# A two-layer encoder trunk: the loads of x wait for the first weights, idle products stand around the last column sums, and the last factor is broadcast into two banks

## The chip, the core and the metric

The kernel runs on one core of one Trainium2 chip. The metric is the device time of one execution in microseconds (us). A core has a matrix engine (TensorE, "PE" in the profile, its weight loads "PEld"), a vector engine (VectorE, "DVE"), a scalar engine (ScalarE, "ACT"), a general engine (GpSimd, "POOL"), and an engine that only issues transfers (SyncE, "SP"). ACT and POOL issue transfers too, from the same instruction stream in which their other work stands; a "q" behind an engine's name (SPq, ACTq, PEq) means this stream. All transfers of the core run on the same 16 DMA engines, in queues: q1 holds what SP issues, q10 what ACT issues.

## The reference

The model width is D = 2048, the sequence S = 256, and there are two layers. Cut to what matters here:

```python
h = x
for i in range(2):
    u = rmsnorm(h, norm_g[i]) @ w_in[i]               # conv group, attention group, gates
    ya, yb = conv_group(u), window_attention(u)       # each times its own gate
    h = h + concat([ya, yb]) @ w_out[i]
    e = rmsnorm(p[i] @ w_pe[i], pe_g[i])              # per-layer embedding, p[i] is (256, 256)
    h = h + e * sigmoid(h @ w_pg[i])
return rmsnorm(h, final_g)

def rmsnorm(x, g):
    return x * rsqrt(mean(x * x, axis=-1) + 1e-6) * g
```

## The kernel before

Activations lie transposed in memory: 128 channels on the partitions, then 16 channel tiles, then the 256 sequence positions. Weights come from memory in half chunks of 512 KB (128 partitions x 1024 floats) in the order in which they are used; two halves make one buffer `raw`, and there are three such buffers. The large products split each weight into a rounded part and a remainder (L163 on ACT, L166 on DVE) and use three passes (L394, L395, L396). The program order on TensorE, VectorE and ScalarE is the order of the code ("manual" order). The order on SP, on POOL and between the transfer queues is set by a planner, which also gives every transfer a semaphore that its landing raises.

The start, which the change touches. VectorE clears a tile `zeros`, and TensorE runs four products on it (`warm`, L256, two instructions each). SP issues `p` (256 KB, L260), then the first weights in seven pieces (L269): the first half in two pieces of 256 KB (`load_half(0, 0, 2)`), the second, third and fourth half in one each; then `gains`, the fifth and sixth half, and small tables. ScalarE runs a small activation `first` (L279) ahead of which its function table is loaded, and issues the four loads of x (512 KB each, L272, queue q10).

TensorE then computes `e = p[0] @ w_pe[0]` straight from the raw weights (L490): eight banks of eight instructions each. The first two banks need the first half (one 256 KB piece each), the next two the second half, and so on. Between the banks ScalarE squares x two tiles at a time (L377, L380, L498), VectorE adds the squares into `hacc` (L381) and folds them at the end (L368), and ScalarE copies each bank of e out (L514). After the fifth bank, `rstd_col` (L343) sums the squares over the channels: products with x's squares as the weights and a column of ones, which give one number per position. DVE scales it (L346), POOL raises it to the power -1/2 (L348), DVE puts it on a diagonal (L353), and `rstd_row` (L359) multiplies a matrix of ones with that diagonal, which broadcasts the factor to all partitions (`rh0b`). The sixth bank of e lies between the two on TensorE. VectorE multiplies x by its gain and this factor (L463, `hn`), ScalarE and VectorE split that into `hg` (L466, L467), and the first large product `ag` begins.

The end, which the change touches too. The last gate product `g` ends; ScalarE and VectorE form the last tile of h and its square (`sq`, L807); `rstd_col` sums over `hparts`, two parts: the folded squares of the tiles before, and this last square. Three products on constants (`warm2`, L845) stand between `rstd_col` and `rstd_row`. The factor `rb` stays in the PSUM bank: VectorE multiplies six of the eight pairs of output tiles by it straight from the bank (L853), ScalarE copies it to `rbs` for POOL (L855), which can't read PSUM and does the other two pairs. Each finished piece is sent out by SP or ScalarE (L856).

Of the kernel before, what the change touches and what calls it, by code (L numbers as in the profile page):

```python
# [12 lines left out]
AF = mybir.ActivationFunctionType  # L13
# [4 lines left out]
P = 128  # L18
D = 2048
# [106 lines left out]
def trunk_kernel(ctx: ExitStack, tc: tile.TileContext, xT, pT, wst, par, gain, relb, sinkp, onehot, out):  # L126
    nc = tc.nc
# [18 lines left out]
    def bank(name):  # L146
        return ps.tile([P, 2, S], F32, tag="ps", name=name)
# [3 lines left out]
    raws, spl = {}, {}  # L151
# [100 lines left out]
    zeros = wk.tile([P, S], F32, name="zeros", tag="sq", bufs=3)  # L252
    nc.vector.memset(zeros, 0.0)
    wb = bank("warm")
# [21 lines left out]
    load_half(0, 0, 2)  # L276

    first = wk.tile([P, 2], F32, name="first", tag="rv")
    nc.scalar.activation(first, zeros[:, 0:2], AF.Square)  # L279
    for k in range(0, KT, 4):  # L280
        load_x(k)
    load_half(0, 1)
# [16 lines left out]
    ident = cst.tile([P, P], F32, name="ident")  # L299
    make_identity(nc, ident)  # L300
    ones = cst.tile([P, P], F32, name="ones")
# [33 lines left out]
        return t  # L335


    def rstd_col(parts, dim, name, between=None):

        c = bank(name + "c")  # L340
        for x, a in enumerate(parts):
            for b in range(2):
                nc.tensor.matmul(c[:, 0, b:b + 1], a[:, b * P:(b + 1) * P], ones[:, 0:1],  # L343
                                 start=(x == 0 and b == 0), stop=(x == len(parts) - 1), skip_group_check=True)
        v = wk.tile([P, 2], F32, name=name + "v", tag="rv")
        nc.vector.tensor_scalar(v, c[:, 0, 0:2], 1.0 / dim, EPS, ALU.mult, ALU.add)  # L346
        col = wk.tile([P, 2], F32, name=name + "col", tag="rcol")
        nc.gpsimd.tensor_tensor(col, v, mhalf, ALU.pow)  # L348
        if between:
            between()  # L350
        dg = wk.tile([P, 2, P], F32, name=name + "dg", tag="rdg", bufs=1)
        for b in range(2):
            nc.vector.tensor_scalar(dg[:, b, :], ident, col[:, b:b + 1], None, ALU.mult)  # L353
        return dg

    def rstd_row(dg, name, tag="rb", copy=True):

        bb = bank(name + "b")
        nc.tensor.matmul(bb[:, 0, :], ones, dg.rearrange("p a b -> p (a b)"), start=True, stop=True)  # L359
        if not copy:  # L360
            return bb[:, 0, :]
        rb = wk.tile([P, S], F32, name=name + "rb", tag=tag, bufs=1)
        nc.scalar.copy(rb, bb[:, 0, :])
        return rb

    def fold(a):
        t = wk.tile([P, S], F32, name="fold", tag="sg")
        nc.vector.tensor_add(t, a[:, 0, :], a[:, 1, :])  # L368
        return t

    def halves_of(a):
        return [a[:, 0, :], a[:, 1, :]]
# [74 lines left out]
    for l in range(DEPTH):  # L447
# [5 lines left out]
        rbs, subs = [], []  # L453
# [21 lines left out]
        for q in range(4):  # L475
            n = Cursor.h
# [5 lines left out]
            for jj in range(0, 4, 2):  # L482
                j = 4 * q + jj
                b = bank("e")
                for x in range(2):
                    for k in range(2):
                        if l:
                            mm3(b[:, x, :], w[:, :, jj + x, k, :], pp[:, :, k, :], x == 0 and k == 0, k == 1)
                        else:
                            nc.tensor.matmul(b[:, x, :], raw[:, jj + x, k, :], pf[:, k, :], start=x == 0 and k == 0,  # L490
                                             stop=k == 1, skip_group_check=True)
                if l == 0 and j // 2 < 4:
# [3 lines left out]
                    if j // 2 == 3:  # L496
                        sq = wk.tile([P, 2, S], F32, name="sq", tag="sq", bufs=3)
                        nc.scalar.activation(sq, h[1][:, 6:8, :], AF.Square)  # L498
                        hparts = [fold(hacc)] + halves_of(sq)
                if j // 2 == QQ[l][0]:  # L500
                    dg = rstd_col(hparts, D, f"rh{l}")
                    ahead(4 if l == 0 else Cursor.h - 1 - q + 5)
# [17 lines left out]
        def embed(l=l, eacc=eacc, e=e):  # L520

            if l == 0:
                yield from wait(8)
                bias_prep()
            for j in range(0, KT, 2):
                yield from wait(2)
                square_acc(eacc, e[j // 8][:, j % 8:j % 8 + 2, :], j == 0)
            yield from wait(6)
            es = fold(eacc)
            yield from wait(3)  # L530
            dg = rstd_col([es], D, f"re{l}")
            yield from wait(2)
            eb = rstd_row(dg, f"re{l}", "reb")
            yield from wait(50)
            while not state["enorm"]:
                yield
            for j in range(KT):
                d = e[j // 8][:, j % 8, :]
                nc.vector.scalar_tensor_tensor(d, d, pcol(l, PO_PE + j), eb, ALU.mult, ALU.mult)
                yield  # L540
# [58 lines left out]
        for q in range(4):  # L599
            n = Cursor.h  # L600
# [96 lines left out]
        def lnorm(l=l, acc=acc, za=za, ya=ya, ysum=ysum, done=done):  # L697
# [10 lines left out]
            for t in range(4):  # L708
                nc.vector.tensor_sub(q[t], q[t], bcast2(mu))
                square_acc(vacc, q[t], t == 0, nc.vector)  # L710
                if t % 2:
                    yield
            yield from wait(LY[0])
            dg = rstd_col(halves_of(vacc), W_CONV, f"rv{l}")
            yield from wait(LY[1])
            rb = rstd_row(dg, f"rv{l}")
# [106 lines left out]
        hparts = []  # L823
# [14 lines left out]
        h = e  # L838


    dg = rstd_col(hparts, D, "rf")

    wb = bank("warm2")
    for _ in range(3):
        nc.tensor.matmul(wb[:, 0, 0:P], ones, ident, start=True, stop=True)  # L845
    rb = rstd_row(dg, "rf", copy=False)
    rbs = wk.tile([P, S], F32, name="rfrb", tag="rb", bufs=1)

    for j in (0, 2, 12, 4, 6, 14, 8, 10):
        for x in [slice(0, 1), slice(1, 2)] if j == 0 else [slice(0, 2)]:  # L850
            d = og[j // 8][:, j % 8:j % 8 + 2, :][:, x, :]
            eng, r = (nc.gpsimd, rbs) if j >= 12 else (nc.vector, rb)
            eng.tensor_mul(d, d, r.unsqueeze(1).broadcast_to(d.shape))  # L853
            if j == 0 and x.start == 0:
                nc.scalar.copy(rbs, rb)  # L855
            (nc.scalar if j >= 12 or j % 4 == 0 and x.start == 0 else nc.sync).dma_start(out[:, j:j + 2, :][:, x, :], d)  # L856


# [75 lines left out]
```

## Time and profile before

| | us |
|---|---|
| median of three runs | 983.94 (983.38 to 984.1) |
| the profiled execution | 983.99 |
| its span, from the first to the last instruction | 982.2 |
| around the span | 1.8 |
| TensorE busy | 965.8 |
| VectorE busy | 774.6 |
| ScalarE busy | 560.0 |
| GpSimd busy | 86.6 |

The mean granted clock of TensorE is 0.992 of full speed. A row of the timeline has the start in us, the length in us, the engine, the line, the operation, what is written and read, and a count where several instructions stand merged in one row; brackets at its end hold the idle time before it and what ended it. A row of a stretch has its length, the busy time of each engine with the number of its instructions, the granted clock ("PEclk"), the mean busy share of the DMA engines and GB/s.

### The profile page before, as it was taken

To read this page: it belongs to the slowest core of one execution; us is meant where nothing else is said; L and a number is where in the kernel's file an instruction comes from. 1 tells how busy PE (TensorE), PEld (TensorE's weight loads), DVE (VectorE), ACT (ScalarE), POOL (GpSimd) and SP (SyncE) were. 2 spreads that over 40 slices of the span, in tenths; PEclk is the share of its full clock that TensorE was granted. 3 is DMA by queue.
4 is the path that set the end of the run, shared out by engine and by line. 5 is a ranking of instruction groups with operands and counts; after the bars stand their busy time and mean duration, and the time that the engine had idled before them with its cause. 6 is when DMAs were issued, how large, how long until landed. Compare 5 with 4: busy or idle time off the path is not lost.

```text
span 982.2 us, 18152 instructions
## 1 busy us (share of the span) xinstructions
PE 965.8 (98%) x7438; PEld 925.5 (94%) x7438; DVE 774.6 (79%) x1319; ACT 560.0 (57%) x862; POOL 86.6 (9%) x87
## 2 busy tenths in 40 slices
PE   8999999999999999999999999999999999999994
PEld 7999999999999999988899999999999999998884
DVE  4899989987787576687789998988887867667763
ACT  4655454777875554455566444568778545446551
POOL 0022001010000000011103200000100000100111
PEclk9999999999999999999999999999999999999997
DMA  7764636555544466446556555456454445654522
GB/s 287 254 238 171 213 131 215 189 178 181 166 153 177 149 238 225 172 172 230 198 184 237 175 203 181 172 188 204 146 168 165 172 143 200 217 191 162 197 104 86
DMA packets 29135, 182.49 MB, mean 186 GB/s; under 512 B 3723, under 2 KB 4284, under 8 KB 9212
## 3 DMA queue, kind: packets, MB, share of 16 engines
q1 hardware_dynamic: 24284, 165.17, 47.2%
q0 software_dynamic: 3472, 12.88, 4.4%
q10 hardware_dynamic: 1296, 3.28, 0.9%
q8 instruction: 58, 0.95, 0.4%
q14 instruction: 25, 0.20, 0.1%
HBM read 177.09 MB, written 4.23 MB: 185 GB/s over the span
## 4 chain that ended last, share of the span: by engine, by line
PE 97%; DVE 1%; DMA 1%; ACT 0%; POOL 0%; issue 0%; DVEq 0%; SPq 0%; ACTq 0%
PE g L391 12%; PE o L394 6%; PE o L395 6%; PE o L396 6%; PE ag L396 6%; PE ag L394 6%; PE ag L395 6%; PE g L392 6%; PE za L394 3%; PE zb L394 3%; PE q L394 3%; PE q L395 3%; PE zb L395 3%; PE za L395 3%; PE zb L396 3%; PE q L396 3%
## 5 line engine op out<-in xcount | busy, mean ns | idle before, releaser
L166 DVE TENSOR_TENSOR w<-raw,w 128x1024 fp32r<-128x1024 f32 x306 | 372.3, 1227 | 119.1 <-ACT w L163 116.1
L163 ACT CAST w<-raw 128x1024 fp32r<-128x1024 f32 x308 | 316.2, 1047 | 180.2 <-PE ag L396 45.1
L560 DVE SCALAR_TENSOR_TENSOR ac<-ac,pars 128x241 f32<-128x241 f32 (+11 forms) x480 | 217.9, 503 | 1.0
L391 PE MATMUL g<-h,w 128*128 128x512 f32 x496 | 175.3, 399 | 0.0
L396 PE MATMUL ag<-hg,w 128*128 128x256 f32 x512 | 145.2, 284 | 0.5 <-DVE w L166 0.5
L394 PE MATMUL ag<-hg,w 128*128 128x256 f32 x512 | 145.5, 284 | 0.0
L395 PE MATMUL ag<-hg,w 128*128 128x256 f32 x512 | 145.1, 283 | 0.1
L392 PE MATMUL g<-h,w 128*128 128x256 f32 x496 | 139.3, 281 | 0.0
L391 PEld LDWEIGHTS g<-h,w 128*128 128x128 f32 x496 | 93.2, 188 | 23.1
L394 PEld LDWEIGHTS ag<-hg,w 128*128 128x128 f32 x512 | 98.3, 192 | 0.9 <-ACT ac L553 0.9
L396 PEld LDWEIGHTS ag<-hg,w 128*128 128x128 f32 x512 | 98.3, 192 | 0.8 <-DVE w L166 0.7
L395 PEld LDWEIGHTS ag<-hg,w 128*128 128x128 f32 x512 | 98.3, 192 | 0.3 <-DVE hg L467 0.3
L392 PEld LDWEIGHTS g<-h,w 128*128 128x128 f32 x496 | 93.8, 189 | 0.0
L394 PE MATMUL za<-hg,w 128*128 128x256 f32 x256 | 73.7, 288 | 0.0
L394 PE MATMUL o<-yb,w 128*128 128x256 f32 x256 | 73.4, 287 | 0.0
L394 PE MATMUL q<-hg,w 128*128 128x256 f32 x256 | 73.3, 286 | 0.0
L394 PE MATMUL zb<-hg,w 128*128 128x256 f32 x256 | 73.2, 286 | 0.0
L395 PE MATMUL o<-yb,w 128*128 128x256 f32 x256 | 72.6, 284 | 0.0
L396 PE MATMUL o<-ya,w 128*128 128x256 f32 x256 | 72.5, 283 | 0.0
L394 PE MATMUL o<-ya,w 128*128 128x256 f32 x256 | 72.5, 283 | 0.0
L395 PE MATMUL o<-ya,w 128*128 128x256 f32 x256 | 72.5, 283 | 0.0
L396 PE MATMUL o<-yb,w 128*128 128x256 f32 x256 | 72.5, 283 | 0.0
(229 smaller groups left out, 2192.9 us busy)
## 6 DMA issues: line engine op xcount, KB each, us to landing
raw<-in_wst SPq DMA_DIRECT2D x153, 1024.0 KB, 4.9
bias<-fscr POOLq DMA_DIRECT2D x16, 384.0 KB, 3.8
raw<-in_wst SPq DMA_DIRECT2D x5, 512.0 KB, 9.8
x<-in_xT ACTq DMA_DIRECT2D x4, 512.0 KB, 7.1
hx<-in_xT POOLq DMA_DIRECT2D x8, 256.0 KB, 3.6
hscr<-e POOLq DMA_DIRECT2D x2, 1024.0 KB, 4.9
hx<-hscr POOLq DMA_DIRECT2D x8, 256.0 KB, 3.4
out_t<-og ACTq DMA_DIRECT2D x4, 256.0 KB, 3.0
```

What stands on the lines that cost most here:

```text
L163: nc.scalar.copy(hi, raw)
L166: nc.vector.tensor_sub(lo, raw, hi.bitcast(F32))
L391: nc.tensor.matmul(o, w[:, 0], x, start=start, stop=False, skip_group_check=True)
L392: nc.tensor.matmul(o[:, 1], w[:, 1], x[:, 0], start=False, stop=stop, skip_group_check=True)
L394: nc.tensor.matmul(o, w[:, 0], x[:, 0], start=start, stop=False, skip_group_check=True)
L395: nc.tensor.matmul(o, w[:, 0], x[:, 1], start=False, stop=False, skip_group_check=True)
L396: nc.tensor.matmul(o, w[:, 1], x[:, 0], start=False, stop=stop, skip_group_check=True)
L560: nc.vector.scalar_tensor_tensor(acc[:, t, lo_:hi_], a[:, t, lo_ + s:hi_ + s], w(k), acc[:, t, lo_:hi_], ALU.mult, ALU.add)
```

## The change

Three edits. The small activation `first` reads two elements of the first weights instead of `zeros`, so that it and all that stands behind it in ScalarE's stream wait until that piece of 256 KB has landed; the four loads of x stand right behind it. In the last norm, `rstd_col` runs five products on constants between its two parts, and four stand behind it where three stood. The factor's broadcast is made twice, into two PSUM banks: VectorE reads the one, ScalarE copies the other for GpSimd.

```diff
     first = wk.tile([P, 2], F32, name="first", tag="rv")
-    nc.scalar.activation(first, zeros[:, 0:2], AF.Square)
+    nc.scalar.activation(first, raws[0][:, 0, 0:2], AF.Square)
     for k in range(0, KT, 4):
         load_x(k)

+    def idle(n):
+        wb = bank("idle")
+        for _ in range(n):
+            nc.tensor.matmul(wb[:, 0, 0:P], ones, ident, start=True, stop=True)
+
-    def rstd_col(parts, dim, name, between=None):
+    def rstd_col(parts, dim, name, between=None, idles=0):
         c = bank(name + "c")
         for x, a in enumerate(parts):
             for b in range(2):
                 nc.tensor.matmul(c[:, 0, b:b + 1], a[:, b * P:(b + 1) * P], ones[:, 0:1],
                                  start=(x == 0 and b == 0), stop=(x == len(parts) - 1), skip_group_check=True)
+            if x == 0 and idles:
+                idle(idles)

-    dg = rstd_col(hparts, D, "rf")
-
-    wb = bank("warm2")
-    for _ in range(3):
-        nc.tensor.matmul(wb[:, 0, 0:P], ones, ident, start=True, stop=True)
+    dg = rstd_col(hparts, D, "rf", idles=5)
+    idle(4)
     rb = rstd_row(dg, "rf", copy=False)
+    rb2 = rstd_row(dg, "rf2", copy=False)
     rbs = wk.tile([P, S], F32, name="rfrb", tag="rb", bufs=1)

             if j == 0 and x.start == 0:
-                nc.scalar.copy(rbs, rb)
+                nc.scalar.copy(rbs, rb2)
```

## Prediction

> **What bounds the kernel now.** I read the page's busy times and its chain first, then the chain and the timeline of the first 25 us and of the last 20, then the transfers and the clock there.
>
> ```profile
> PE 965.8 (98%) x7438; PEld 925.5 (94%) x7438; DVE 774.6 (79%) x1319; ACT 560.0 (57%) x862; POOL 86.6 (9%) x87
> PE 97%; DVE 1%; DMA 1%; ACT 0%; POOL 0%; issue 0%; DVEq 0%; SPq 0%; ACTq 0%
> PE ag L396 <- DVE w L166: 0.5, 1, 0.5
> ```
>
> TensorE is busy 98% of the span and is 97% of the chain. The third row is from the waits of TensorE: between the start of `ag` and the last norm it lists this one and no longer one. So a delay at the start goes to the end undiminished, and the change can only move the first 25 us and the last 16.
>
> The start, from the timeline:
>
> ```profile
> 0.74 0.39 SPq L260 DMA_DIRECT2D p<-in_pT  x1
> 1.19 3.62 PE L256 MATMUL warm<-zeros 128*128 128x256 f32 x8 [1.19 <-DVE zeros L253]
> 7.07 10.56 PE L490 MATMUL e<-p,raw 128*128 128x256 f32 x40 [2.25 <-DMA raw<-in_wst]
> 14.69 0.63 ACT L380 ACTIVATE sq<-x 128x512 f32<-128x512 f32 x1
> 16.08 0.42 DVE L368 TENSOR_TENSOR fold<-hacc 128x256 f32<-128x256 f32 x1
> 17.46 0.50 PE L343 MATMUL rh0c<-ones,fold 128*128 128x1 f32 x4
> 17.82 1.03 PE L343 MATMUL rh0c<-ones,sq 128*128 128x1 f32 x8
> 18.89 0.16 DVE L346 TENSOR_SCALAR rh0v<-rh0c 128x2 f32<-128x2 f32 x1 [2.39 <-PE rh0c L343]
> 20.52 0.65 PE L359 MATMUL rh0b<-rh0dg,ones 128*128 128x256 f32 x2
> 21.01 3.62 PE L490 MATMUL e<-p,raw 128*128 128x256 f32 x16
> 24.27 0.47 PE L394 MATMUL ag<-hg,w 128*128 128x256 f32 x1
> ```
>
> The warm products end at 4.81, and TensorE waits 2.25 us for the first weights. The five banks of e take it to 17.6. The sum of squares (fold) is ready at 16.50, so here TensorE is late by about 1 us and the statistics of x are not. Behind it `rh0c`, the power, `rh0b` and `ag` follow.
>
> The transfers and the clock. The first row is the line that issues x, with the times of its first and last issue; then the queues from 1.7 to 3, from 2.7 to 13.6, from 7 to 13 (two rows) and from 13 to 15 (packets, MB, share); then from issue to landing; then stretches:
>
> ```profile
> L272 ACTq DMA_DIRECT2D x<-in_xT x4: 334/416/453, 1.2 to 7.0; - x4
> q10 hardware_dynamic: 10, 0.04, 11.1%
> q10 hardware_dynamic: 576, 2.10, 51.8%
> q10 hardware_dynamic: 344, 1.25, 52.2%
> q1 hardware_dynamic: 382, 1.21, 50.3%
> q1 hardware_dynamic: 354, 0.79, 102.9%
> x<-in_xT ACTq DMA_DIRECT2D x4, 512.0 KB, 7.1
> p<-in_pT SPq DMA_DIRECT2D x1, 256.0 KB, 2.8
> 4.53:7.94 3.41, 1.16 (x6) 0.83 (x5) 0.00 (x0) 0.61 (x2) 0.00 (x0) 1.00 0.85 269
> 7.95:11.35 3.40, 3.40 (x9) 2.65 (x9) 0.89 (x2) 1.88 (x5) 0.00 (x0) 0.50 1.03 421
> 11.35:17.60 6.25, 6.25 (x31) 5.49 (x31) 3.68 (x6) 4.85 (x9) 0.00 (x0) 1.00 1.03 405
> ```
>
> All of x (2.10 MB) moves in the 10.9 us from 2.7 to 13.6. Between 7 and 13 both queues have work and halve the bandwidth: 1.25 and 1.21 MB in 6 us, 0.21 MB per us each; q1 nearly alone, from 13 to 15, has 0.39. A stretch of 3.41 us in which TensorE was busy only 1.16 is followed by 3.4 us at clock 0.50.
>
> The end, from the timeline and two stretches:
>
> ```profile
> 966.80 0.50 PE L343 MATMUL rfc<-ones,fold 128*128 128x1 f32 x4
> 968.92 0.61 PE L343 MATMUL rfc<-ones,sq 128*128 128x1 f32 x4 [1.62 <-ACT sq L807]
> 969.39 0.92 PE L845 MATMUL warm<-ident,ones 128*128 128x128 f32 x6
> 970.55 0.48 DVE L353 TENSOR_SCALAR rfdg<-ident,rfcol 128x128 f32<-128x128 f32 x2 [0.82 <-POOL rfcol L348]
> 971.18 1.19 PE L359 MATMUL rfb<-rfdg,ones 128*128 128x256 f32 x2 [0.88 <-DVE rfdg L353]
> 972.40 0.42 DVE L853 TENSOR_TENSOR og<-og,rfb 128x256 f32<-128x256 f32 x1 [1.38 <-PE rfb L359]
> 972.86 0.37 ACT L855 COPY rfrb<-rfb 128x256 f32<-128x256 f32 x1 [3.60 <-DVE og L853]
> 973.26 3.41 DVE L853 TENSOR_TENSOR og<-og,rfb 128x256 f32<-128x256 f32 x6 [0.44 <-ACT rfrb L855]
> 973.31 2.49 POOL L853 TENSOR_TENSOR og<-og,rfrb 128x512 f32<-128x512 f32 x2 [2.80 <-ACT rfrb L855]
> 967.33:970.74 3.41, 1.38 (x10) 1.19 (x10) 1.20 (x4) 0.93 (x3) 0.71 (x1) 0.97 0.00 0
> 970.74:973.00 2.26, 1.19 (x2) 0.50 (x2) 0.71 (x3) 0.14 (x1) 0.00 (x0) 0.50 0.00 0
> 976.00:980.00 4.00, 0.00 (x0) 0.00 (x0) 0.67 (x2) 0.00 (x0) 0.00 (x0) 0.50 1.02 378
> ```
>
> TensorE is busy 1.38 of 3.41 us, and then the clock is 0.50: the broadcast takes 1.19 us where the same one at the start, at full clock, took 0.65. VectorE, ScalarE and VectorE then read one bank in turn. From 976 on the output transfers fill the DMA engines (1.02).
>
> **Part one, the loads of x.** Nothing is removed; four issues of 512 KB and all of ScalarE's stream behind `first` wait for the first 256 KB of weights. The function table is loaded ahead of `first` and stays. POOL and SP don't stand behind the wait.
>
> When do these weights land? `p`, equally large and ahead on the same queue, was issued at 0.74 and landed 2.8 later, at 3.5. Without x, q1 has the engines to itself; 256 KB more at 0.39 MB per us are 0.7 us: 4.2, and I take 4.4. Then `e` starts at the end of the warm products, 4.8 instead of 7.07, and has no gap ahead of it, so the half clock of 7.95 to 11.35 goes too. 40 instructions at 3.62/16 = 0.226 us are 9.0: the fifth bank ends at 13.9 instead of 17.6. Its later weights come in time: landed at 3.5, `p` (0.26 MB) had moved by about 3.0, so by 5.4, when x starts, q1 has moved 0.26 + 2.4 x 0.39 = 1.2 MB; it needs 1.3 MB for the third bank (at 8.4) and 1.8 MB for the fifth (at 12.0), and at 0.21 MB per us these are there at 5.9 and 8.3, half a microsecond more for the landing.
>
> What is late next is x. Issued at 4.4, its first bytes move about 1 us later, at 5.4 (an estimate: issued at 1.2, x had moved 0.04 MB by 3.0, which bounds it at 1.7). SP still has some 2.3 MB of weights queued (six halves of 0.52 MB and `p` make 3.4), so the two queues halve the bandwidth until x is through: 2.10/0.21 = 10.0 us, 15.4. In the run above the last load of x, issued at 7.0, landed 7.1 later, at about 14.05, 0.5 behind its last bytes at 13.6, so now 15.9, 1.9 later. From the second to last square (14.69) to the end of the fold (16.50) pass 1.81: the sums can begin at 15.9 + 0.1 + 1.8 = 17.8 instead of 17.46. That is +0.35, and TensorE, done at 13.9, waits 3.9 us for it.
>
> That wait has a price. As at 4.53 to 7.94, a stretch of 3.41 us with little work gives 3.4 us at half clock, and now the twelve sums (1.39 us at full clock), the sixth bank (1.8) and the broadcast lie in it. Upper bound: half clock all the way, the twelve cost 1.3 more, and the sixth bank outlasts the power chain (18.89 to 20.47) by 1 us: +2.3. Lower bound: the edge of the stretch falls such that the clock is back when the sums start: 0. I take 1.3, since only part of the 3.4 us meets work. Part one is +1.65; its ends are -1.4 (x lands when it did, the clock stays; the sums then start at 16.0) and +4 (below).
>
> The Trainium skill, "TensorE: Matmul & The Clock Gate", Part 1, has the clock halved after one idle window of about 3.4 us, and advises no idle gap over some 3 us. By the letter of that the last 1.6 us gap before 970.74 should have cost nothing; the trace shows 0.50, so the share of busy time decides here, and the measurement goes. With the letter, a wait of 3.9 us costs the same 1.3, but one of under 3 us nothing, and the sum would be 983.4.
>
> The same skill's "DMA: Bandwidth & Descriptors", Queues, rings and completion order, says that each DMA engine goes round between queues packet by packet; the 1.25 against 1.21 MB agree, and it speaks against the gain that holding x back is to bring: SP's later weights, not needed for 10 us, take half of what x then gets.
>
> **Part two, the idle products.** Five products, ten instructions at 0.92/6 = 0.15 us, are 1.5 us: from 967.3 to 968.8, inside the wait that ends at 968.92. If they ran long, each 0.1 us would be on the path. Four behind are eight instructions, 1.2 us from 969.4: 970.6, covered by the power and the diagonal up to 971.03. TensorE is then busy some 2.9 of 3.4 us, the clock stays, and the broadcast takes 0.65 instead of 1.19: -0.54. Bound from below 0, if the edge falls otherwise.
>
> **Part three, the second bank.** Two more instructions behind the first broadcast, 0.45 us, before ScalarE's copy: POOL starts at about 972.7 instead of 973.31. VectorE no longer waits for that copy (0.44) nor for turns at the bank: its second piece goes at 972.25 instead of 973.26. All but the first output are about 1.0 earlier by parts two and three together, the first 0.54. Since the transfers are the limit from 976 on, the end moves by between 0.54 and 1.0; I take 0.9.
>
> Sum against the profiled execution's own 983.99 (0.05 above the median): 983.99 + 0.35 + 1.3 - 0.9 = 984.7.
>
> **The rivals.**
>
> *Slower: x is planned behind all of SP's loads.* A transfer's issue can wait for an older landing:
>
> ```profile
> SPq L286 <- DMA raw<-in_wst: 5.4, 1, 5.4
> SPq L269 <- DMA p<-in_pT: 0.5, 1, 0.5
> ```
>
> With `p` and these `raw` pieces and x, about eight transfers were out when issues began to wait; the fourth x, too, was issued only at 7.0, when the first weights had landed. If the planner now counts SP's thirteen before x, the first x waits for the fourth `raw` half (2.4 MB, landed at about 9) and the last for the sixth, near 12.8; ScalarE's squares stand behind that. x then lands at 18 to 19.5, the sums start at 20 to 21.4: +2.5 to +4 and the clock's 1.3, less 0.9: 987.5. It decides from a first issue of x after about 6 us on. For it: the waits above. Against it: before, x was issued among SP's loads, from 1.2 on, and not behind them.
>
> *Neutral: the clock stays and x gets more than half.* Before, x moved ahead of the small-packet weights early on. If x lands near 15, the sums start at 17.0: 983.99 - 0.5 - 0.9 + some clock = 983.0.
>
> *Faster.* x lands at 14.1 and the clock stays: 983.99 - 1.4 - 0.9 = 981.7. Against it: x starts to move 2.7 us later and would need 2.10 MB in 8.2 us, 0.26 MB per us, where it had 0.21.
>
> *The idle products change nothing*, because the edge of the 3.4 us falls elsewhere: 0.5 of the gain goes, 985.2. The skill's clock page has this window run free of the kernel.
>
> **How the numbers follow.** Forecast 0.45, neutral 0.18, slower rival 0.20, idle products without effect 0.07, faster 0.10. What this measurement can tell from no change is about 0.2%, 2.0 us: faster is below 982.0, the last case and a little of neutral, 0.12; slower is above 985.9, the rival and the forecast's upper tail (half clock throughout, 985.7, and x later), 0.26; the rest, 0.62, is the same. The forecast's own range is 983.5 to 986.2. The range for 8 in 10 leaves out most of the faster case and the worst of the rival: 982.2 to 987.6.
>
> **What would show it.** In the trace after: ScalarE's issues of x at 4.2 to 4.6; `e` at about 4.8 and its first forty instructions done near 13.9; then a wait of TensorE for ScalarE or VectorE before `rh0c`, which starts between 17.3 and 18.5, at clock 0.50 for part of what follows; `ag` 1 to 2.5 us after 24.27. At the end clock 1.00 to the broadcast, `rfb` in some 0.65, VectorE's products without the gap before the second. I am wrong if `rh0c` starts before 16.8 or after 19.5, or if `rfb` still takes 1.19.

## The result, and the profile after

The changed kernel takes 990.74 us (990.55 to 991.15, five runs) against 983.94 before: 1.007 times as long, with a 95% interval of 1.0056 to 1.0084. The forecast was 984.7 with a range of 982.2 to 987.6, and no measurable difference as the likeliest outcome. The profiled execution takes 990.70, its span 988.9.

The timeline of TensorE after the change, from the start to the first large product:

```profile
1.19 3.50 PE L256 MATMUL warm<-zeros 128*128 128x256 f32 x8 [1.19 <-DVE zeros L253]
5.33 3.69 PE L498 MATMUL e<-p,raw 128*128 128x256 f32 x16 [0.65 <-DMA raw<-in_wst]
9.37 5.45 PE L498 MATMUL e<-p,raw 128*128 128x256 f32 x24 [0.35 <-DMA raw<-in_wst]
22.69 1.02 PE L349 MATMUL rh0c<-ones,fold 128*128 128x1 f32 x4 [7.87 <-DVE fold L376]
23.57 1.84 PE L349 MATMUL rh0c<-ones,sq 128*128 128x1 f32 x8
25.27 3.39 PE L498 MATMUL e<-p,raw 128*128 128x256 f32 x8
28.50 0.59 PE L367 MATMUL rh0b<-rh0dg,ones 128*128 128x256 f32 x2
...
32.20 0.47 PE L402 MATMUL ag<-hg,w 128*128 128x256 f32 x1
```

`e` starts 1.74 earlier than before (5.33 for 7.07) and its five banks end at 14.8 instead of 17.6. All of that is lost in one wait: TensorE stands 7.87 us until the fold of x's squares is there. `rh0c` starts at 22.69 instead of 17.46, 5.23 later. From `rh0c` to `ag` pass 9.51 instead of 6.81, so `ag` is 7.93 later.

ScalarE's timeline says what the fold waited for:

```profile
5.22 0.20 ACT L279 ACTIVATE first<-raw 128x2 f32<-128x2 f32 x1 [3.20 <-DMA raw<-in_wst]
5.22 6.26 ACTq L272 DMA_DIRECT2D x<-in_xT  x4
13.68 0.63 ACT L385 ACTIVATE hacc<-x 128x512 f32<-128x512 f32 x1 [8.26 <-DMA x<-in_xT]
...
20.82 0.63 ACT L388 ACTIVATE sq<-x 128x512 f32<-128x512 f32 x1 [1.05 <-DMA x<-in_xT]
```

x is issued from 5.22 on. The first load lands 8.4 us later, at 13.66, and the last at 20.74; the last squares begin at 20.82.

The queues (packets, MB, share of the DMA engines) in the stretches 5 to 8.8, 8.8 to 9 (the row of q10), 9 to 13 (two rows) and 13 to 17 (two), and the row from issue to landing:

```profile
q1 hardware_dynamic: 363, 1.23, 96.2%
...
q10 hardware_dynamic: 3, 0.01, 14.9%
...
q10 hardware_dynamic: 212, 0.82, 58.7%
q1 hardware_dynamic: 286, 0.62, 43.1%
...
q10 hardware_dynamic: 245, 0.87, 55.5%
q1 hardware_dynamic: 225, 0.75, 46.4%
...
x<-in_xT ACTq DMA_DIRECT2D x4, 512.0 KB, 9.6
```

From 5 to 8.8 there is no row of q10 at all, although x has been issued since 5.22: SP's queue has the engines alone. The first packets of x move at 8.87, 3.65 after the issue. From then to 17 the queues share as before: (0.82 + 0.87) MB in 8 us are 0.21 MB per us for x. From 17 to 20.2, to its last bytes, x has 0.40 MB, 0.13 per us, beside 0.75 MB of weights.

The clock, in the stretches 15 to 17.9, 17.9 to 22.69 and 22.69 to 28.1:

```profile
15.00:17.90 2.90, 0.00 (x0) 0.00 (x0) 1.94 (x3) 1.93 (x4) 0.00 (x0) 1.00 1.03 420
17.90:22.69 4.79, 0.00 (x0) 0.00 (x1) 2.50 (x4) 3.49 (x7) 0.00 (x0) 0.50 0.89 307
22.69:28.10 5.41, 5.41 (x19) 4.87 (x20) 1.77 (x4) 2.13 (x3) 0.70 (x1) 0.50 0.04 17
```

It is granted at 0.50 for 10 us, 5.4 of them with TensorE busy without a gap. The end, from the timeline:

```profile
974.51 0.50 PE L349 MATMUL rfc<-ones,fold 128*128 128x1 f32 x4
...
974.88 1.36 PE L342 MATMUL idle<-ident,ones 128*128 128x128 f32 x10
...
976.64 0.60 PE L349 MATMUL rfc<-ones,sq 128*128 128x1 f32 x4 [0.41 <-ACT sq L815]
...
977.11 1.14 PE L342 MATMUL idle<-ident,ones 128*128 128x128 f32 x8
...
978.90 0.67 PE L367 MATMUL rfb<-rfdg,ones 128*128 128x256 f32 x2 [0.65 <-DVE rfdg L361]
...
979.40 0.59 PE L367 MATMUL rf2b<-rfdg,ones 128*128 128x256 f32 x2
979.60 3.74 DVE L859 TENSOR_TENSOR og<-og,rfb 128x256 f32<-128x256 f32 x7 [0.85 <-PE rfb L367]
980.03 0.37 ACT L861 COPY rfrb<-rf2b 128x256 f32<-128x256 f32 x1 [3.05 <-PE rf2b L367]
...
980.48 2.49 POOL L859 TENSOR_TENSOR og<-og,rfrb 128x512 f32<-128x512 f32 x2 [2.25 <-ACT rfrb L861]
```

The broadcast takes 0.67 instead of 1.19, and VectorE's seven products go without the gap. From the first `rfc` to the end of the span pass 14.4 us (988.9 less 974.51) instead of 15.4.

So +7.7 up to the first `rfc` (974.51 for 966.80) and -1.0 behind it make the +6.7 of the two profiled executions.

One of the eleven executions of `end_only`, told below, took 2414.79 us; its ratio is worked out without it.

### The profile page after: what moved, and what is told of

Read it like the earlier page. It is cut to its first block, busy times and chain, and to the rows that moved or that the text cites. A ratio compares the mean times of both kernels' runs of the same rounds, so it can differ in the third digit from the quotient of the medians.

```text
span 988.9 us, 18181 instructions
## 1 busy us (share of the span) xinstructions
PE 968.4 (98%) x7452; PEld 928.0 (94%) x7452; DVE 774.5 (78%) x1319; ACT 559.8 (57%) x862; POOL 86.6 (9%) x87
## 4 chain that ended last, share of the span: by engine, by line
PE 95%; DMA 2%; DVE 1%; ACT 0%; SPq 0%; issue 0%; POOL 0%; DVEq 0%; ACTq 0%
PE g L399 12%; PE o L402 6%; PE o L403 6%; PE o L404 6%; PE ag L404 6%; PE ag L402 6%; PE ag L403 6%; PE g L400 6%; PE za L402 3%; PE zb L402 3%; PE q L402 3%; PE zb L403 3%; PE q L403 3%; PE za L403 3%; PE q L404 3%; PE zb L404 3%
```

## The experiments

Each is told with the median of its runs and the ratio to runs of the kernel before on the same chip, with the 95% interval; those runs had medians of 983.9 to 984.05.

### Which part loses the time

**The loads alone** (`gate_only`), the kernel before with one line changed:

```diff
-    nc.scalar.activation(first, zeros[:, 0:2], AF.Square)
+    nc.scalar.activation(first, raws[0][:, 0, 0:2], AF.Square)
```

> Part one alone: ScalarE's first activation reads the first weights, the end is that of the kernel before. Theory (the whole loss is at the start and the end gains about 1.05 us): rfc starts 7.7 us later than before, the time is 983.9 + 7.7 = 991.6. Rival (the end's edits have a part in the loss): 990.7 or less, and rfc starts less than 7 us later.

992.12 us (four runs), 1.0076 (1.006 to 1.0091). `rh0c` starts at 22.66, behind a wait of 7.64 for the fold, and the first `rfc` at 975.28, 8.5 later than before. One line is the whole loss. It is 0.8 more than in the changed kernel (7.7), since the half clock lasts until 30.53 here instead of 28.16: from `rh0c` to `ag` pass 10.70 us instead of 9.51.

**The end alone** (`end_only`): the changed kernel with `zeros` back in that line.

> Parts two and three alone; ScalarE's first activation reads zeros as before. Theory: from the first rfc to the end of the span 14.4 us instead of 15.4, the time 982.9. Rival (the gain belongs to the other phase of the clock and not to the edits): 983.9, 15.4 us.

983.02 us, 0.9992 (0.9983 to 1.0001). From the first `rfc`, at 966.80, to the end pass 14.5 us, so the end's gain is there without part one. TensorE's timeline at the start shows besides what bounds `e`:

```profile
6.97 1.97 PE L498 MATMUL e<-p,raw 128*128 128x256 f32 x8 [2.00 <-DMA raw<-in_wst]
9.67 1.99 PE L498 MATMUL e<-p,raw 128*128 128x256 f32 x8 [0.73 <-DMA raw<-in_wst]
12.19 5.45 PE L498 MATMUL e<-p,raw 128*128 128x256 f32 x24 [0.53 <-DMA raw<-in_wst]
```

Here the products run at full pace and wait for the second piece of weights and for the second half instead. They end where they ended before (17.6), where some had run at half clock: the half clock at the start of the kernel before mostly covered these landings.

**The idle products alone** (`idle_only`) **and the second bank alone** (`bank_only`), each the kernel before with part two or part three of the diff.

> Part two alone: x as before, the idle products at the end, one bank for the factor. Theory (the gain of 0.9 us in the span of the two end parts is half the clock's): clock 1.00 at rfb, rfb 0.65 instead of 1.19, VectorE's second product still waits for ScalarE's copy (0.44); from the first rfc to the end of the span 14.9 instead of 15.4, the time 983.4. Rival (all of it is the clock): 14.4, 982.9.

> Part three alone: x as before, three idle products behind the sums as before, the factor broadcast into two banks. Theory: rfb at clock 0.50 takes 1.19 as before where the clock's edge falls as before, VectorE's second product follows the first without a gap, ScalarE's copy waits for the second broadcast, some 1.2 us at half clock; from the first rfc to the end 14.9 to 15.2, the time 983.5. Rival (POOL's later start at half clock eats it): 15.4, 983.9.

`idle_only`: 983.42 us, 0.9992 (0.9984 to 1.0001); from the first `rfc` (967.94) to the end of the span (982.8) 14.9 us. VectorE's timeline, with the gap behind the first product that the shared bank makes:

```profile
973.03 0.42 DVE L858 TENSOR_TENSOR og<-og,rfb 128x256 f32<-128x256 f32 x1 [0.85 <-PE rfb L367]
973.89 3.41 DVE L858 TENSOR_TENSOR og<-og,rfb 128x256 f32<-128x256 f32 x6 [0.44 <-ACT rfrb L860]
```

`bank_only`: 983.87 us, 0.9998 (0.9989 to 1.0007); from the first `rfc` (967.04) to the end (982.4) 15.4 us, as before. Its timelines of TensorE, VectorE and GpSimd:

```profile
971.42 1.19 PE L359 MATMUL rfb<-rfdg,ones 128*128 128x256 f32 x2 [0.87 <-DVE rfdg L353]
972.40 1.06 PE L359 MATMUL rf2b<-rfdg,ones 128*128 128x256 f32 x2
...
972.64 3.74 DVE L854 TENSOR_TENSOR og<-og,rfb 128x256 f32<-128x256 f32 x7 [1.38 <-PE rfb L359]
...
973.95 2.49 POOL L854 TENSOR_TENSOR og<-og,rfrb 128x512 f32<-128x512 f32 x2 [3.19 <-ACT rfrb L856]
```

At half clock the second broadcast takes 1.06. VectorE's gap is gone, but GpSimd starts 6.9 us behind the first `rfc` instead of 6.5 before. So of the end's 0.9 to 1.0 the idle products alone bring 0.5, the second bank alone nothing that shows, and the rest comes only where the second broadcast is made at full clock. These are lengths in one profiled execution each; the intervals of the three ratios all reach 1.

### Why x came so late

**The weights held back** (`x_ahead`): the changed kernel, with the second and third pair of halves (the third to sixth half) issued only after ScalarE's four loads of x; the first, 1.31 MB with `p`, as before. SP's order is that of the code here, not the planner's.

```diff
     for k in range(0, KT, 4):
         load_x(k)
+    for c in (1, 2):
+        raws[c] = wraw.tile([P, 2, HALF], F32, tag="raw", name=f"raw{c}")
+        for x in range(2):
+            nc.scalar.activation(raws[c][:, x, 0:2], zeros[:, 0:2], AF.Square)
     load_half(0, 1)
```

> The changed kernel, but the third to sixth half of the weights are issued only once ScalarE has issued all four loads of x (small activations behind those issues write into their buffers first; SP keeps the order of the code). x is still issued at about 5.2. Theory (x stood behind the weights that SP had issued before it): x moves its first bytes within 1.7 us of its issue, x lands by 13 to 16, rh0c starts at 16 to 17.5, the time is 983.0 to 985.5. Rival (a late first issue of its queue costs 3.7 us by itself, or the halved bandwidth is all there is): first bytes at 8.9 again, rh0c not before 19, the time 987 or more.

984.72 us, 1.0006 (0.9996 to 1.0017). x is issued at 5.55 and its first bytes move at 6.58, 1.0 later: this is the delay that the prediction had taken. Its loads land from 9.97 to 16.84. The queues from 6.5 to 8 (two rows) and from 8 to 12 (two), and two rows of TensorE:

```profile
q10 hardware_dynamic: 81, 0.33, 76.4%
q1 hardware_dynamic: 23, 0.06, 10.2%
...
q10 hardware_dynamic: 351, 1.27, 98.2%
q1 hardware_dynamic: 2, 0.01, 1.8%
...
16.59 1.97 PE L502 MATMUL e<-p,raw 128*128 128x256 f32 x8 [1.51 <-DMA raw<-in_wst]
18.80 0.61 PE L353 MATMUL rh0c<-ones,fold 128*128 128x1 f32 x4 [0.24 <-DVE fold L380]
```

It is the mirror image. The weights issued from 7.97 on, behind x, move their first bytes at 11.63, land at 16.46, and now the fifth bank of `e` waits for them and ends at 18.56. `rh0c` starts at 18.80, later than I had expected (16 to 17.5): it waits for the fold, 0.24 us behind that bank, since from 12 on the weights take turns with x, whose last load lands at 16.85. So the weights' delay, with which I hadn't reckoned, doesn't set this start alone: x, too, took 10.3 us from its first bytes to its last landing.

**Another kind of queue** (`gate_pool`): x issued by GpSimd, on its software queue q0, each load behind a small copy that reads the first weights.

```diff
-        nc.scalar.dma_start(h[k // 8][:, k % 8:k % 8 + 4, :], xT[:, k:k + 4, :])
+        nc.gpsimd.tensor_copy(h[k // 8][:, k % 8, 0:2], raws[0][:, 0, 0:2])
+        nc.gpsimd.dma_start(h[k // 8][:, k % 8:k % 8 + 4, :], xT[:, k:k + 4, :])
```

> The kernel with both end parts; x is issued by GpSimd on its own queue, behind small GpSimd copies that read the first weights (so at about 5.5), and ScalarE's first activation reads zeros. SP has its weights queued as in the changed kernel. Theory (what SP has issued holds back what ScalarE issues after it; GpSimd's queue is fed another way): x moves its first bytes within 2.5 us of its issue, by 8.0, while SP's queue still moves weights, and the two then share as the prediction had it: x landed at 16.5 to 18.5, rh0c at 18.4 to 20.4, the time 985 to 988. Rival (x gets nothing until the weights issued before it are through, on whatever queue): first bytes at 8.9 or later, rh0c at 22 or more, the time 988.5 or more.

991.96 us, 1.0076 (1.0062 to 1.009), `rh0c` at 23.61: the theory that only SP's and ScalarE's queues hold each other back has fallen, and the rival's numbers came. The queues from 6 to 10, and from 10 to 11 (two rows):

```profile
q1 hardware_dynamic: 366, 1.12, 95.4%
...
q1 hardware_dynamic: 95, 0.29, 93.1%
q0 software_dynamic: 8, 0.03, 8.5%
```

Issued at 6.10, x moves from 10.40 on. Its four issues stand at 6.10 to 7.90 without a wait, and the last lands at 21.64, 11.2 us behind the first bytes; after the change, where the fourth issue waited until 11.15 for a landing, that distance is 11.9. So this wait cost some 0.6 us at most.

**Smaller rows** (`gate_2k`): the later weights in pieces of 256 KB with rows of 2 KB.

> The changed kernel with the second to fourth half of the weights issued in pieces of 256 KB (rows of 2 KB instead of 4), so that what stands queued ahead of x has twice the rows for the same bytes. Looked at is only when x moves its first bytes (later loads of x wait for older landings here). Theory (the engines have taken in a fixed number of rows, about 14 each, of the queue that was there first): 0.45 MB instead of 0.9 move between the issue of x and its first bytes, which come at 7.0 to 7.6. Rival (bytes, or all that was issued ahead): 0.8 MB or more, first bytes at 8.3 or later.

991.22 us (one run). x, issued at 5.00, moves from 9.46 on. About 0.99 MB of weights move in between, twice as much as a fixed number of rows would give, so the number of rows isn't what is waited for.

**Half of x at once** (`gate_half`): the first two loads of x issued at the start, the others behind the first weights.

```diff
+    load_x(0)
+    load_x(4)
     nc.scalar.activation(first, raws[0][:, 0, 0:2], AF.Square)
-    for k in range(0, KT, 4):
-        load_x(k)
+    load_x(8)
+    load_x(12)
```

> Both end parts; ScalarE issues x's first two loads at once and only the last two behind the activation that waits for the first weights (so at about 6.9). At that time the second to fourth half of the weights have been issued ahead of them, as in the changed kernel. Theory (a queue that already moves goes on taking its turns, only one that starts cold behind another's backlog waits): the third load lands at 11 to 11.8 and the fourth at 13.8 to 14.8, as before, rh0c at 17.3 to 17.9, the time 983.0. Rival (whatever was issued ahead, on any queue, moves first): the third load lands after the fourth half of the weights, at 14 or later, the fourth at 16 or later, rh0c at 18.5 or more, the time 984.5 or more.

984.9 us, 1.0009 (1.0 to 1.0018). With x ahead the first weights land only at 8.33, so the third load is issued at 8.36. ScalarE's queue had run dry by then (its last bytes moved at 8.32), so the condition of my theory (a queue that still moves) was not met. The third load's first bytes move at 11.53, it lands at 14.70 and the fourth at 17.28, and `rh0c` starts at 19.23, waiting for the fold: these are the rival's numbers.

The packets up to each issue and up to the first bytes, with what the other queue had been given before it, make one table. A piece issued within 0.02 us ahead of x (in `after`, `gate_2k` and `gate_half`) isn't counted as ahead.

| | issued | still to move of what was issued ahead, MB | moved until the first bytes, MB | delay, us |
|---|---|---|---|---|
| before | 1.18 | 0.26 | 0.17 | 1.6 |
| `x_ahead` | 5.55 | 0.30 | 0.25 | 1.0 |
| `x_ahead`, weights behind x | 7.97 | 1.77 | 1.17 | 3.7 |
| `gate_half`, third load | 8.36 | 1.44 | 1.33 | 3.2 |
| after | 5.22 | 1.67 | 1.21 | 3.65 |
| `gate_pool` | 6.10 | 1.90 | 1.23 | 4.3 |
| `gate_2k` | 5.00 | 1.28 | 0.99 | 4.5 |

`gate_only` and `gate_filled`, whose start is that of the changed kernel, have 1.03 of 1.66 MB in 3.6 us and 1.09 of 1.61 MB in 3.5. A fixed delay of a queue's start is excluded (1.0 to 4.5). What the rows share: a queue that has nothing to move when its transfer is issued gets its first packets after some six to nine tenths of what was issued ahead of it elsewhere has moved. A queue that is moving takes turns: in the kernel before, the fourth x was issued at 6.95 and landed at 14.08, ahead of weights issued at 3.58 (15.48). Why it isn't all of what is ahead isn't shown. A part of the answer may be that the sixteen DMA engines aren't level. In the changed kernel the last weights counted as ahead of x (issued at 3.07) landed on the first engine at 9.31 and on the last at 13.16, and x's first packet came at 8.87, when the first engine was nearly through with them. In `before`, `gate_only`, `gate_filled`, `gate_2k` and `gate_half`, too, x's first packet came 0.2 to 0.9 us ahead of the first landing of the last weights (`p` in `before`) issued ahead of it. That would fit a line that each engine keeps for itself; no run tests it, and `gate_pool` (10.40, between first landings at 9.53 and 11.88) doesn't decide.

### What the wait cost in clock

**The wait filled** (`gate_filled`): the changed kernel with 34 idle products between the fifth bank and `rh0c`.

> The changed kernel, with 34 idle products (68 instructions) on TensorE between the fifth bank of e and the first column sums, in the 7.9 us that TensorE waits there. Theory (the half clock after the wait costs 2.4 us): clock 1.00 at rh0c, the twelve sums in 1.4 instead of 2.7 us, rh0c's start unchanged at 22.7, the time 988.3. Rival (the wait alone is the loss and the power chain hides the half clock): 990.0 to 990.7.

988.68 us, 1.0043 (1.003 to 1.0057). TensorE's timeline:

```profile
14.96 7.75 PE L342 MATMUL idle<-ident,ones 128*128 128x128 f32 x68
22.55 0.52 PE L349 MATMUL rh0c<-ones,fold 128*128 128x1 f32 x4
22.93 1.03 PE L349 MATMUL rh0c<-ones,sq 128*128 128x1 f32 x8
...
25.64 0.65 PE L367 MATMUL rh0b<-rh0dg,ones 128*128 128x256 f32 x2
...
29.39 0.47 PE L402 MATMUL ag<-hg,w 128*128 128x256 f32 x1
```

The sums start when they did (22.55 for 22.69), and from there to `ag` pass 6.84 instead of 9.51. The half clock was worth 2.1 (by the medians) to 2.7 us; the other 5 us are x.

### Is there a better start

**One queue** (`one_queue_end`): both edits of the end, x issued by SP in the order of need: the first half of the weights, two loads of x, the second half, the other two.

> A version that should beat both: the two end parts, and x issued by SP itself in the order of need (p, the first half, x's first two loads, the second half, x's last two, then the rest). Theory (the order of issue is the order of movement): x landed at about 12.5, the third bank of e at 9 to 9.5, the fifth at about 14, rh0c at 15.5 to 16 instead of 17.46, clock 1.00, the time 981 to 981.7. Rival (a single queue moves no more than 0.33 MB per us early on, and the fifth bank's weights come too late): rh0c at 17.5 or later, 983.

983.10 us, 0.9987 (0.9978 to 0.9996), not the 981 to 981.7 expected but the rival's 983, with 0.29 MB per us on the one queue from 3 to 9. `e` starts at 4.83 and x is through by 14.95, but

```profile
12.47 5.81 PE L500 MATMUL e<-p,raw 128*128 128x256 f32 x24 [2.68 <-DMA raw<-in_wst]
```

the second half, issued at 3.06, lands on the first of the sixteen DMA engines at 9.29 and on the last at 12.43, and the third bank waits for the last. `rh0c` starts at 18.12.

**The first half in one load** (`whole_first_end`): both edits of the end, `load_half(0, 0)` for `load_half(0, 0, 2)`.

> Both end parts, x as before, the first half of the weights in one load (rows of 4 KB instead of 2). Theory (in turns packet by packet, rows of 2 KB got half of what x's rows of 4 KB got): the first weights land at 7.5 to 8.2 instead of 6.9, the second half at 10.4 to 11.2 instead of 11.9, the fifth bank of e ends about 0.8 earlier, rh0c at 16.5 to 16.9, the time 982.2. Rival (the later first landing is not made up): rh0c at 17.5 or later, 983.0 or more.

984.77 us, 1.0005 (0.9996 to 1.0014), a miss. The landings came as the theory had them or earlier (the first half at 7.59, the second at 10.07), but TensorE has a gap of 2.75 us and then goes slowly:

```profile
7.72 11.83 PE L498 MATMUL e<-p,raw 128*128 128x256 f32 x40 [2.75 <-DMA raw<-in_wst]
```

Forty instructions take 11.83 instead of 9.0 and wait for nothing: they start 0.43 us apart until 13.8 and 0.22 apart from there on. The trace's first record of the granted clock is at 13.71 in this run, and it is 1.00; what the profile shows ahead of it (1.00 too) rests on no record. The first warm products stand 0.43 apart as well, in every run here. So TensorE seems to have gone at half clock from its start to 13.71, where the kernel before has its first record of 1.00 at 4.53 and falls to 0.50 only behind the gap. That it is the clock is an inference from the pace.

**More warm products** (`warm9_end`): both edits of the end, and TensorE kept busy until the first weights.

```diff
-NWARM = 4
+NWARM = 9
```

> The two edits at the end, and nine warm products at the start instead of four (eighteen instructions instead of eight, ending near 7.0 instead of 4.9), so that TensorE has no gap before the first weights. Theory: in the kernel with the end edits alone the first products stand between the weights' landings, and the rest of its scatter is the half clock that follows the 2 us gap and falls on e in some runs. With no gap the clock stays at 1.00 from 5 on, rh0c starts at 17.4 to 17.6 in every run: 982.9, nearly all runs between 982.5 and 983.5. Rival: the scatter comes from when the sixteen engines land their pieces, not from the clock: the same median, 983.0, and the same spread up to 985. Second rival: the warm products run on behind the landing and delay e by some tenths: 983.2 to 983.6.

982.85 us, 0.9989 (0.998 to 0.9998), eleven runs from 982.71 to 983.10, where `end_only` had 982.83 to 985.04. TensorE's timeline:

```profile
1.19 6.51 PE L256 MATMUL warm<-zeros 128*128 128x256 f32 x18 [1.19 <-DVE zeros L253]
7.54 3.70 PE L498 MATMUL e<-p,raw 128*128 128x256 f32 x16
11.82 5.45 PE L498 MATMUL e<-p,raw 128*128 128x256 f32 x24 [0.58 <-DMA raw<-in_wst]
17.11 0.50 PE L349 MATMUL rh0c<-ones,fold 128*128 128x1 f32 x4
```

No gap, full pace (the warm products go from 0.43 to 0.22 us apart at 6.03, with this trace's first record of the clock at 6.01), and the scatter falls to 0.4 us, as the theory said. What it takes away shows in the profiled execution of `idle_only`, the slowest of its eleven (984.63, median 983.42): behind a gap of 2.06 us the forty products take 11.74 us, 0.43 apart until the first record of the clock, at 12.85. The median gains only 0.2 on `end_only`, because the landing of the second half (11.8) still bounds `e`. This version, `end_only` and `one_queue_end` (982.85, 983.02 and 983.10) are all about 1 us faster than before and are the best of those that ran; of `end_only` the interval just reaches 1. So it is the end that gains, and of the starts only the nine warm products add something, 0.2 us and less scatter. They were not run together with the first half in one load.

## Why the prediction was wrong

- **x's first bytes, the step that failed.** "Issued at 4.4, its first bytes move about 1 us later, at 5.4" took the delay from the kernel before, where x started with 0.26 MB ahead of it. Here 1.67 MB were ahead, and the first bytes moved at 8.87. Of the 4.84 us by which the last x landed after my 15.9, 0.8 are the first weights (5.19 instead of 4.4), 2.65 this delay (3.65 instead of 1.0), and the remaining 1.4 stand behind the first bytes: 11.9 us to the last landing where the working had 10.5. `x_ahead` shows the step itself to be the cause: with little ahead the delay is 1.0.
- **What had moved by then was too much**: the working let q1 alone move 0.39 MB per us from 3.0 on, the rate of 13 to 15. From 3 to 5.22 it moved 0.37 MB, 0.17 per us; the first weights landed 0.8 later than forecast, and by 5.22 only 0.71 MB had moved where the working gives some 1.1.
- **The rate was right up to 17**: 0.21 MB per us for x from 9 on; behind that x had 0.13 per us, and that makes up most of the 1.4. The working from the last x to `rh0c` was right, 1.9 us forecast, 1.95 measured.
- **The clock's price was too small**, 1.3 with a bound of 2.3; it measured 2.1 to 2.7. That a wait brings the half clock held, but I had taken it to last 3.4 us whatever the wait; behind a wait twice as long as forecast it lasted from 17.92 to 28.16, 10.24 us, three times 3.41. The Trainium skill, "TensorE: Matmul & The Clock Gate", Why this matters for your kernels, warns of idle gaps of more than some 3 us between bursts; the trace agrees, since the clock falls to 0.50 at 17.92, 3.1 us behind the last product, and the filled wait keeps `rh0c` at full pace.
- **The rule on turns was read too far.** "DMA: Bandwidth & Descriptors", Queues, rings and completion order, in the Trainium skill has each DMA engine go round the queues that have work, packet by packet. For two moving queues the trace agrees (0.87 and 0.75 MB from 13 to 17); for a queue that starts behind another's issued transfers the turns don't begin with the issue: none against 1.23 MB from 5 to 8.8. Whether x's pieces had reached the engines by then, no run shows.
- **The slower rival** came out on the right side by another way. Its mechanism, x's issue waiting for SP's landings, was to decide from a first issue after 6; that came at 5.22. Only the fourth waited, until 11.15, and that cost at most some 0.6.
- **`e`** started at 5.33 for 4.8 and its fifth bank ended at 14.8 for 13.9; neither mattered, since TensorE then waited 7.87 (3.9 forecast). My sign of a wrong forecast, `rh0c` after 19.5, came true.
- **The end was right**: 0.9 forecast, 0.9 (`end_only`) to 1.0 measured; the idle products 0.54 forecast, 0.5 measured; the broadcast 0.65 forecast, 0.67 measured. Part three's share of it comes only together with part two (`bank_only`).

In one sum: `ag` was to be 1.65 later and is 7.93 later, 4.9 of the 6.3 between by x's landing and 1.4 by the clock; 0.2 of it is regained on the way to the end.

## What to carry to other kernels

Before holding a transfer back so that another may go first, count what else will have been issued by the time it starts: in these runs a queue with nothing in motion waited for most of that, and only a queue already moving took turns. To give one load the right of way, hold back the bulk that isn't needed yet, or put both in one queue in the order of need, and not the transfer that the next long wait depends on. Here both took the loss away, and neither was faster than issuing all at once (`x_ahead` 984.72, `one_queue_end` 983.10, `end_only` 983.02). The wait of 7.9 us on TensorE was paid twice, once as time and once as half clock behind it; idle products in the wait saved the second payment. Gaps of 2.25 us (before) and 2.75 us (`whole_first_end`), too, had products at half pace behind them, one of 2.0 us in `end_only` didn't.

## What the runs showed of the hardware that I had not expected

- A queue that starts dry behind another's transfers moved nothing for 3.2 to 4.5 us (while 0.99 to 1.33 MB of the others moved); GpSimd's software queue behaved as the others did (4.3).
- After 7.9 us without a product the half clock went on for 5.4 us of unbroken products. At the start of these runs it lasted 3.41 us behind gaps of 2.25, 2.40 and 3.50 us (before, `bank_only`, `gate_half`) and 10.24 us behind gaps of 6.6 to 8.6 us (after, `gate_only`, `gate_pool`, `gate_2k`), although in `gate_only` two of its three stretches of 3.41 us were full of products.
- One load of 512 KB doesn't land at once: its sixteen parts came 3.1 us apart in `one_queue_end` (9.29 to 12.43) and 3.9 after the change (9.31 to 13.16), and the reader waits for the last.
- Where a trace has no record of the clock yet, the profile shows 1.00, and the pace of the products (0.43 us apart, not 0.22) tells otherwise.
- A kernel's scatter of some 2 us from run to run came down to 0.4 us when TensorE had no gap at the start.
